# Gate banks of the first three column pairs copied at once, raw weights loaded two pairs ahead, and down weights scaled apart from their splits, in a decoder layer on one core

## Chip, cores and metric

The kernel runs on one core of a Trainium2 chip. The metric is the device time of one execution in microseconds (us); lower is better. Three runs of the kernel before gave 1916.0, 1916.4 and 1918.68 us, median 1916.4.

## What is computed

A decoder layer on 1024 tokens of width 1024 in float32: an attention mixer and a SwiGLU feed-forward, each followed by a residual and a layer norm. The change lies in the feed-forward and in the layer norm just ahead of it.

```python
D_MODEL, SEQ, D_FF = 1024, 1024, 2816

def swiglu(u, w_gate_up, w_down):
    h = jnp.einsum('btd,df->btf', u, w_gate_up)
    hg, hu = jnp.split(h, 2, axis=-1)
    return jnp.einsum('btf,fd->btd', jax.nn.silu(hg) * hu, w_down)

def reference(...):
    ...
    x = layer_norm(DEEPNORM_ALPHA * x + (1.0 + gate_m) * y, ln1_g[l], ln1_b[l])
    u = x * (1.0 + scale_f) + shift_f
    y = swiglu(u, w_gate_up[l], w_down[l])
    return layer_norm(DEEPNORM_ALPHA * x + (1.0 + gate_f) * y, ln2_g[l], ln2_b[l])
```

## The kernel before

**Split operands.** TensorE multiplies in a reduced float32 form, so each operand is held as a high part and a low part. ScalarE copies the source to the high part (L112, L73, L1042), VectorE subtracts to get the low part (L113, L74, L1043), and a product takes three matmuls: high by high, high by low, low by high. Every split is thus one ScalarE and one VectorE instruction on the same tile.

**Gate and up.** The hidden width of 2816 is worked through in 22 pairs p of 128 gate columns and 128 up columns. Gate and up together, for the two halves of the tokens and the two halves of the width, make a 2x2 block product, and it is done with seven products of blocks in place of eight (a form of Strassen's scheme). The names of the seven moving operands are, in order of i = 0 to 6: b11, b21, t2, t1, t3, b22, t4. Each product is 12 matmuls of 128x512 (`product`, L1102). The products accumulate in three PSUM banks in the order a, b, a, c, a, c, a, so bank a is written at i = 0, 2, 4 and 6. Between two of these its value so far has to be read out: ScalarE copies it after i = 0 and after i = 2 (L1236), after i = 4 (L1244), and bank c after i = 3 (L1244). Bank b is added by VectorE at i = 1 (L1247) and a Silu follows (L1248). At i = 6 VectorE multiplies gate by up twice (L1252, L1253), and two stores put the hidden activations into DRAM (`h_d`, L1255).

**Weights of a pair.** `g_load(p)` loads two raw tiles of 512 KB, r1 and r2, two buffers each (L1060, L1064). `g_sums(p, ·)` makes the sums on GpSimd: s1 (L1076), s2 (L1078), a new r2 (L1080), and, when split (p,5) is prepared, a new r1 (L1082). `g_split` splits the right one for each product, some two products ahead. From p = 2 on the next pair's load is written at i = 2 of the current pair, for p = 1 at i = 0; pair 1's own load is early.

**The first three pairs.** Products i = 0 and 1 of pairs 0, 1 and 2 run early, between the last tiles of the layer norm, and leave their sums in six banks. While they run, the second half of the normalized input is transposed (`late_input(k)`, k = 0 to 3), and operands t2, t1, t3, b22 and t4 are made from it piece by piece on ScalarE, VectorE and GpSimd (`late_rest`). Then the loop over p starts and does i = 2 to 6 of pairs 0, 1 and 2, and all seven from pair 3. In it, bank a of a pair is copied only when that pair's turn comes. Tiles of the pool x2p are in use up to the end of pair 0; the pool ev takes that memory from pair 1 on.

**The change of phase.** In pair 21 the loop begins on the down projection: `h_load(f)` loads hidden tiles back, `h_prepare(f)` splits them, and `ws.step()` does a piece of the down weights: GpSimd scales it (L68), ScalarE and VectorE split it (L73, L74). The pieces have three raw buffers, of which each is sent again once its split is done.

**Gain.** In pairs 3 to 10, at i = 6, GpSimd applies the first layer norm's gain and bias to one tile (`gain`, L1023, L1024), from the tile gb1, which is loaded ahead of the layer norm (L961).

**Order.** The schedule is manual: every engine runs its instructions in the order in which the code writes them, and waits for each in turn.

## Time and profile before

| | |
|---|---|
| median of three runs | 1916.4 us |
| the profiled execution | 1917.84 us |
| its span in the trace | 1916.0 us |
| PE (TensorE) busy in the span | 1844.8 us, 96% |
| DVE (VectorE) busy | 1180.4 us, 62% |
| ACT (ScalarE) busy | 781.3 us, 41% |
| POOL (GpSimd) busy | 605.2 us, 32% |
| mean granted TensorE clock | 0.988 |

PE is the engine that decides here. What is to be found is therefore the time in which PE does not run or runs at a lower granted clock. The views for that are the busy time by stage with the granted clock, PE's waits with the line that released each, and the timeline of PE and of the engine that released it. In the timeline a bracket gives the idle time ahead of an instruction and what ended it. Consecutive matmuls overlap, so their spacing, not their duration, is what one costs.

### The profile page before, as it was taken

The page shows a single profiled execution, that of the slowest core. Times are in us where ns is not written, and L with a number is a line of the kernel's source. Part 1 is how long each engine was busy: PE and PEld are TensorE (multiplying, and loading weights), DVE is VectorE, ACT ScalarE, POOL GpSimd, SP SyncE. Part 2 cuts the span into 40 slices and gives each one's busy share as a digit, 9 for nine tenths or more (in the row PEclk, how much of TensorE's full clock was granted, in tenths as well). Part 3 has the DMA queues.
Part 4 walks back from the last instruction along what each step waited for, and adds up shares of the span by engine and source line. Part 5 has one row for each costly group of instructions (what it writes and reads, how often), then busy time and mean ns, then how long its engine had stood idle before and what let it go on. Part 6 is the DMA issues. An engine that isn't in the chain of part 4 may idle for free.

```text
span 1916.0 us, 24451 instructions
## 1 busy us (share of the span) xinstructions
PE 1844.8 (96%) x8988; PEld 1489.2 (78%) x8988; DVE 1180.4 (62%) x2157; ACT 781.3 (41%) x1661; POOL 605.2 (32%) x393
## 2 busy tenths in 40 slices
PE   6899999999999999989999999979999999999998
PEld 5688877878878767768888878758888888788886
DVE  7755667667677887534455365656766445575557
ACT  3455545445444767633122132643333333422122
POOL 2332223223323222000222141635665434431213
PEclk9899999999999999999999999989999999999999
DMA  8011112111121222255434133112222222442222
GB/s 320 22 34 34 40 38 76 46 57 56 41 67 45 58 83 71 74 191 167 167 127 141 60 108 107 56 66 72 94 70 95 72 94 72 149 141 96 95 75 88
DMA packets 72266, 170.83 MB, mean 89 GB/s; under 512 B 13073, under 2 KB 14161, under 8 KB 72146
## 3 DMA queue, kind: packets, MB, share of 16 engines
q1 hardware_dynamic: 71810, 168.21, 26.3%
q8 instruction: 71, 1.16, 0.2%
q0 software_dynamic: 336, 1.06, 0.2%
q14 instruction: 49, 0.40, 0.1%
HBM read 145.80 MB, written 23.43 MB: 88 GB/s over the span
## 4 chain that ended last, share of the span: by engine, by line
PE 50%; DVE 3%; issue 1%; ACT 1%; DMA 1%; POOL 0%; SPq 0%; DVEq 0%; POOLq 0%; ACTq 0%
PE pf L1102 20%; PE p L133 5%; PE p L134 5%; PE p L132 5%; PE pf L133 5%; PE pf L134 5%; PE pf L132 5%; DVE m L113 1%; DMA h_raw<-h_d 0%; DVE w_lo L113 0%; DMA r<-in_w_gate_up 0%; ACT w_hi L112 0%; DMA w_raw<-in_w_down 0%; POOL w_raw L68 0%; DVE t3l L1043 0%
## 5 line engine op out<-in xcount | busy, mean ns | idle before, releaser
L132 PE MATMUL pj<-u,w_hi 128*128 128x512 f32 x720 | 300.9, 418 | 0.0
L134 PE MATMUL pj<-u,w_lo 128*128 128x512 f32 x720 | 283.5, 394 | 0.0
L133 PE MATMUL pj<-u,w_hi 128*128 128x512 f32 x720 | 282.3, 392 | 0.0
L420 POOL TENSOR_TENSOR rb<-rb,sin_t 128x512 f32<-128x512 f32 x64 | 86.8, 1356 | 502.1 <-DVE rb L418 431.5
L113 DVE TENSOR_TENSOR w_lo<-r,w_hi 128x512 fp32r<-128x512 f32 x110 | 99.9, 917 | 143.3 <-ACT w_hi L112 143.3
L74 DVE TENSOR_TENSOR w_lo<-w_raw,w_hi 128x512 fp32r<-128x512 f32 x150 | 133.2, 891 | 83.0 <-ACT w_hi L73 80.7
L523 ACT ACTIVATE probs<-probs,st 128x128 f32<-128x128 f32 (+1 forms) x320 | 146.1, 461 | 60.7 <-DVE st L513 31.0
L132 PEld LDWEIGHTS pj<-u,w_hi 128*128 128x128 f32 x720 | 136.1, 189 | 33.5 <-issue 4.7
L134 PEld LDWEIGHTS pj<-u,w_lo 128*128 128x128 f32 x720 | 135.7, 188 | 30.6
L133 PEld LDWEIGHTS pj<-u,w_hi 128*128 128x128 f32 x720 | 136.3, 189 | 22.5
L133 PE MATMUL pf<-wd,h 128*128 128x512 f32 x352 | 137.0, 389 | 0.6 <-DVE wd L74 0.6
L132 PE MATMUL pf<-wd,h 128*128 128x512 f32 x352 | 137.2, 390 | 0.0
L134 PE MATMUL pf<-wd,h 128*128 128x512 f32 x352 | 137.0, 389 | 0.0
L68 POOL TENSOR_TENSOR w_raw<-w_raw,gate 128x512 f32<-128x512 f32 x60 | 84.6, 1426 | 155.6 <-DMA w_raw<-in_w_down 141.5
L1307 DVE SCALAR_TENSOR_TENSOR zt<-zt,pf 128x512 f32<-128x512 f32 x112 | 76.0, 686 | 80.2 <-PE pf L134 80.2
L421 POOL TENSOR_TENSOR r<-ra,rb 128x512 f32<-128x512 f32 x63 | 114.5, 1818 | 6.1 <-DVE kl L455 1.3
L73 ACT ACTIVATE w_hi<-w_raw 128x512 fp32r<-128x512 f32 x150 | 92.0, 624 | 29.0 <-PE p L133 12.0
L547 ACT ACTIVATE ptsb<-pt 128x512 f32<-128x512 f32 (+1 forms) x128 | 63.6, 548 | 93.5 <-PE pt L545 93.1
L132 PE MATMUL p<-u,w_hi 128*128 128x512 f32 x224 | 88.3, 394 | 0.0
L134 PE MATMUL p<-u,w_lo 128*128 128x512 f32 x224 | 87.2, 389 | 0.0
L133 PE MATMUL p<-u,w_hi 128*128 128x512 f32 x224 | 87.2, 389 | 0.0
L132 PE MATMUL p<-o_hl,w_hi 128*128 128x512 f32 x192 | 75.8, 395 | 6.1 <-ACT o_hl L112 6.1
(293 smaller groups left out, 4323.7 us busy)
## 6 DMA issues: line engine op xcount, KB each, us to landing
w_raw<-in_w_in SPq DMA_DIRECT2D x118, 256.0 KB
r<-in_w_gate_up SPq DMA_DIRECT2D x47, 512.0 KB
a_raw<-in_w_ada SPq DMA_DIRECT2D x32, 512.0 KB
w_raw<-in_w_down SPq DMA_DIRECT2D x44, 256.0 KB
h_raw<-h_d SPq DMA_DIRECT2D x22, 512.0 KB
h_d<-g SPq DMA_DIRECT2D x42, 256.0 KB
wa<-in_w_ada_m SPq DMA_DIRECT2D x16, 512.0 KB
wb<-wt_d SPq DMA_DIRECT2D x24, 256.0 KB
```

The source lines that it names most:

```text
L68: self.nc.gpsimd.tensor_tensor(raw, raw, scale(), op=OP.mult)
L73: self.nc.scalar.activation(hi, raw, AF.Copy)
L74: self.nc.vector.tensor_tensor(lo, raw, hi, op=OP.subtract)
L113: nc.vector.tensor_tensor(lo, src, hi, op=OP.subtract)
L132: nc.tensor.matmul(ps, w[0], m[0], start=first, stop=False)
L133: nc.tensor.matmul(ps, w[0], m[1], start=False, stop=False)
L134: nc.tensor.matmul(ps, w[1], m[0], start=False, stop=last)
L420: eng.tensor_tensor(b, b, sin_t[:, s], op=OP.mult)
L421: eng.tensor_tensor(residue_half(res, r, t), by_residue(a, r), by_residue(b, r), op=OP.add)
L523: nc.scalar.activation(pr, pr, AF.Exp, bias=st[:, 0, h, b:b + 1], accum_out=st[:, 1, h, b:b + 1])
L1102: nc.tensor.matmul(ps, w[:, c], m[:, k], start=first and k == 0 and n == 0, stop=k == 3 and n == 2, skip_group_check=True)
L1307: nc.vector.scalar_tensor_tensor(z, z, ALPHA if gi == 0 else 1.0, pd, op0=OP.mult, op1=OP.add)
```

## The change

The added function `early_gate(p)` copies bank a of pair p on ScalarE, and adds bank b on VectorE, at once after those banks are complete. It is called for pair 0 after `late_input(0)`, for pair 1 after `late_input(2)`, and for pair 2 at p = 0, i = 2. At i = 0 and 1 of those pairs the copy and the add are then left out; the Silu stays. The results lie in a weight buffer (pair 0) and in a new tile `spare`, which takes the memory of gb1; gb1 is loaded in pair 3 instead. The last two tiles of `late_input` go into `spare` too.

Four subtractions that make raw21 (the source of t4) go from GpSimd to VectorE, between the four low parts of b22.

`g_load(p + 2)` is written at i = 4 of every pair, `g_sums(p + 1, ·)` at i = 2, 3 and 4.

The scaling of a down piece is a method of its own. Three pieces are sent at p = 20, i = 5 and scaled at p = 21, i = 0; the splits are spread over i = 2, 3, 5 and 6.

```diff
+    def scale(self, i):
+        scale = self.jobs[i][2]
+        if scale is not None and i not in self.scaled:
+            self.nc.gpsimd.tensor_tensor(self.raws[i], self.raws[i], scale(), op=OP.mult)
+            self.scaled.add(i)
...
     def step(self):
...
         self.send()
-        _, kh, scale, dest = self.jobs[i]
+        self.scale(i)
+        _, kh, _, dest = self.jobs[i]
         raw = self.raws.pop(i)
-        if scale is not None:
-            self.nc.gpsimd.tensor_tensor(raw, raw, scale(), op=OP.mult)
...
-    gb1 = norm_params(1)
...
+    spare = misc.tile([P, 4, TH], F32, name="spare", tag="gb")
+    late, gated = {}, {}
...
         elif name == "t3":
             split_to("t3", k, r12)
-            nc.gpsimd.tensor_tensor(raw21[:, k], raw21[:, k], raw_t2[:, k], op=OP.subtract)
...
+    def early_gate(p):
+        gated[p] = wpool.tile([P, TH], F32, name="w_raw", tag="w_raw", bufs=3) if p == 0 else spare[:, p - 1]
+        nc.scalar.activation(gated[p], acc[p][0], AF.Copy)
+        nc.vector.tensor_tensor(gated[p], gated[p], acc[p][1], op=OP.add)
...
         if k == 1:
             g_split(0, 2)
+        if k in (0, 2):
+            early_gate(k // 2)
...
             if p == 0 and i == 2:
                 late_rest("t3", 0)
+                early_gate(2)
...
             if i in (0, 2):
-                g[i // 2] = kept("g")
-                nc.scalar.activation(g[i // 2], x, AF.Copy)
+                g[i // 2] = gated.get(p) if i == 0 else None
+                if not g[i // 2]:
+                    g[i // 2] = kept("g")
+                    nc.scalar.activation(g[i // 2], x, AF.Copy)
...
             if i in (1, 5):
                 t = i // 5
-                nc.vector.tensor_tensor(g[t], g[t], x, op=OP.add)
+                if t or p not in gated:
+                    nc.vector.tensor_tensor(g[t], g[t], x, op=OP.add)
                 nc.scalar.activation(g[t], g[t], AF.Silu)
...
             if p == 0 and i in (3, 4):
                 for k in range(4):
+                    if i == 3:
+                        nc.vector.tensor_tensor(raw21[:, k], raw21[:, k], raw_t2[:, k], op=OP.subtract)
                     late_rest({3: "b22", 4: "t4"}[i], k)
             if p + 1 < NF:
-                if i == (2 if p >= EARLY_PAIRS - 1 else 0) and p:
-                    g_load(p + 1)
-                if i in ((3, 4, 5) if p >= EARLY_PAIRS else (2, 3, 4)):
-                    g_sums(p + 1, i - (3 if p >= EARLY_PAIRS else 2))
+                if i == 4 and p + 2 < NF:
+                    g_load(p + 2)
+                if i in (2, 3, 4):
+                    g_sums(p + 1, i - 2)
+                if p == NF - 2 and i == 5:
+                    ws.limit = None
+                    ws.send()
             else:
                 if i == 0:
-                    ws.limit = None
-                    ws.send()
-                if i == 1:
                     h_load(0)
                     h_load(1)
+                    for j in range(3):
+                        ws.scale(len(ws.done) + j)
                 if i in (2, 3, 4):
                     h_prepare(i - 2)
-                    if i < 4:
-                        h_load(i)
+                    if i == 2:
+                        h_load(2)
+                for _ in range({2: 2, 3: 1, 5: 1, 6: 2}.get(i, 0)):
                     ws.step()
-                    ws.step()
+            if p == EARLY_PAIRS and i == 0:
+                gb1 = norm_params(1)
```

In the rows of the instruction order that follow, a line number under "now" is that of the changed file, 4 to 13 higher.

**ScalarE, from the last `late_input` to product t2 of pair 0.** Here `px` is a transposed tile, `pf` a bank, and w_hi the high part of a weight. Before:

```order
L1031 ACTIVATE w_raw<-px,lnpp 128x512 x2
L1042 ACTIVATE t2h<-raw_t_10490 128x512
L1042 ACTIVATE t1h<-raw_10063 128x512 x2
L112 ACTIVATE w_hi<-s_10418 128x512
L1236 ACTIVATE w_raw<-pf 128x512
L1248 ACT_TABLE_LOAD
L1248 ACTIVATE w_raw<-w_raw 128x512
L1042 ACTIVATE t3h<-r 128x512
L1236 ACTIVATE r<-pf 128x512
L1042 ACTIVATE t3h<-r 128x512 x2
```

Now:

```order
L1046 ACTIVATE t1h<-raw_10060 128x512
L1174 ACTIVATE spare<-pf 128x512
L1035 ACTIVATE spare<-px,lnpp 128x512 x2
L1046 ACTIVATE t2h<-raw_t_10487 128x512
L1046 ACTIVATE t1h<-raw_10060 128x512 x2
L117 ACTIVATE w_hi<-s_10415 128x512
L1261 ACT_TABLE_LOAD
L1261 ACTIVATE w_raw<-w_raw 128x512
L1046 ACTIVATE t3h<-r 128x512
L1174 ACTIVATE spare<-pf 128x512
L1248 ACTIVATE r<-pf 128x512
```

The copies of the banks of pairs 1 and 2 stand among the operands' copies, pair 0's stands some rows above, and the table load and the Silu follow the weight split directly.

**VectorE, products t3 to t4 of pair 0**, from the low part of t3's weights. Before:

```order
L113 TENSOR_TENSOR w_lo<-r_10353,w_hi 128x512
L113 TENSOR_TENSOR w_lo<-r_10351,w_hi 128x512
L1043 TENSOR_TENSOR b22l<-r,b22h 128x512 x3
L1043 TENSOR_TENSOR b22l<-w_raw,b22h 128x512
L113 TENSOR_TENSOR w_lo<-r_10353,w_hi 128x512
L1043 TENSOR_TENSOR t4l<-raw_10064,t4h 128x512 x4
L113 TENSOR_TENSOR w_lo<-s_10704,w_hi 128x512
```

Now:

```order
L118 TENSOR_TENSOR w_lo<-r_10350,w_hi 128x512
L118 TENSOR_TENSOR w_lo<-r_10348,w_hi 128x512
L1272 TENSOR_TENSOR raw_10061<-raw_10061,raw_t_10487 128x512
L1047 TENSOR_TENSOR b22l<-r,b22h 128x512
L1272 TENSOR_TENSOR raw_10061<-raw_10061,raw_t_10487 128x512
L1047 TENSOR_TENSOR b22l<-r,b22h 128x512
L1272 TENSOR_TENSOR raw_10061<-raw_10061,raw_t_10487 128x512
L1047 TENSOR_TENSOR b22l<-r,b22h 128x512
L1272 TENSOR_TENSOR raw_10061<-raw_10061,raw_t_10487 128x512
L1047 TENSOR_TENSOR b22l<-spare,b22h 128x512
L118 TENSOR_TENSOR w_lo<-r_10350,w_hi 128x512
L1047 TENSOR_TENSOR t4l<-raw_10061,t4h 128x512 x4
```

The four subtractions that make raw21 (here `raw_1006…`) stand between the low parts of b22.

**SyncE, pairs 0 to 2** (both pieces begin with the two loads of pair 1; the first two stores into `h_d` are pair 0's, the next two pair 1's; each further two loads are those of the next pair). Before:

```order
L1060 DMA r_10523<-in_w_gate_up 128x1024
L1064 DMA r_10525<-in_w_gate_up 128x1024
L1255 DMA h_d<-w_raw 128x512
L1255 DMA h_d<-r 128x512
L1060 DMA r_10807<-in_w_gate_up 128x1024
L1064 DMA r_10809<-in_w_gate_up 128x1024
L1255 DMA h_d<-g 128x512 x2
L1060 DMA r_10935<-in_w_gate_up 128x1024
L1064 DMA r_10937<-in_w_gate_up 128x1024
```

Now:

```order
L1064 DMA r_10521<-in_w_gate_up 128x1024
L1068 DMA r_10523<-in_w_gate_up 128x1024
L1064 DMA r_10762<-in_w_gate_up 128x1024
L1068 DMA r_10764<-in_w_gate_up 128x1024
L1268 DMA h_d<-w_raw 128x512
L1268 DMA h_d<-r 128x512
L1064 DMA r_10871<-in_w_gate_up 128x1024
L1068 DMA r_10873<-in_w_gate_up 128x1024
L1268 DMA h_d<-spare 128x512
L1268 DMA h_d<-g 128x512
L1064 DMA r_10976<-in_w_gate_up 128x1024
L1068 DMA r_10978<-in_w_gate_up 128x1024
```

Pair 2's loads stand ahead of pair 0's stores, pair 3's ahead of pair 1's, and so on: each load has moved up by about one pair.

**ScalarE, end of pair 21** (`wd` is a piece of the down weights, `h` a hidden tile, `c` the copies after i = 3 and i = 4). Before:

```order
L73 ACTIVATE wd<-w_raw 128x512 x2
L112 ACTIVATE w_hi<-r_13507 128x512
L1244 ACTIVATE c_13693<-pf 128x512
L112 ACTIVATE h<-h_raw 128x1024
L73 ACTIVATE wd<-w_raw 128x512 x2
L112 ACTIVATE w_hi<-r_13509 128x512
L1244 ACTIVATE c_13727<-pf 128x512
L112 ACTIVATE h<-h_raw 128x1024
L73 ACTIVATE wd<-w_raw 128x512 x2
L1248 ACTIVATE g<-g 128x512
```

Now:

```order
L78 ACTIVATE wd<-w_raw 128x512 x2
L117 ACTIVATE w_hi<-r_13409 128x512
L1256 ACTIVATE c_13691<-pf 128x512
L117 ACTIVATE h<-h_raw 128x1024
L78 ACTIVATE wd<-w_raw 128x512
L117 ACTIVATE w_hi<-r_13411 128x512
L1256 ACTIVATE c_13717<-pf 128x512
L117 ACTIVATE h<-h_raw 128x1024
L1261 ACTIVATE g<-g 128x512
L78 ACTIVATE wd<-w_raw 128x512 x3
```

Ahead of the split of (21,6) and the second c copy stands one piece in place of two, ahead of the Silu none in place of two, and three follow the Silu.

## Rows read from the trace of the kernel before

**Rows 1.** Busy time by stage: pair 0, pair 1, and the stretch from pair 3 on. The columns are the stretch, its length, the busy time (and instructions) of PE, PE's weight loads, DVE, ACT and POOL, the granted TensorE clock, the share of the DMA engines and GB/s.

```profile
1236.00:1262.00 26.00, 19.67 (x62) 14.06 (x60) 20.59 (x23) 14.57 (x26) 15.28 (x10) 0.80 0.00 1
1262.00:1282.00 20.00, 16.14 (x64) 13.11 (x65) 8.50 (x12) 7.89 (x14) 6.83 (x5) 0.91 0.22 79
1301.00:1640.00 339.00, 339.00 (x1490) 278.87 (x1489) 196.35 (x195) 128.30 (x231) 166.66 (x103) 1.00 0.25 84
```

**Rows 2.** Waits of PE from 1236 us to the end of the span: the waiting line, the line it waited for, us in total, times, longest.

```profile
PE pf L1102 <- ACT c L1244: 6.1, 2, 3.3
PE pf L1102 <- ACT g L1236: 4.0, 1, 4.0
PE pf L1102 <- ACT w_raw L1236: 2.7, 1, 2.7
PE pf L1102 <- ACT w_hi L112: 2.1, 1, 2.1
PE pf L1102 <- DVE w_lo L113: 1.4, 1, 1.4
PE pf L133 <- DVE wd L74: 0.6, 1, 0.6
```

**Rows 3.** Timeline of PE, from the last matmul ahead of pair 0's t2 to pair 3: start, duration, operation, and in brackets the idle time ahead and what ended it.

```profile
1235.87 0.39 PE L1102 MATMUL pf<-b21h,w_lo 128*128 128x512 f32 x1
1238.95 0.50 PE L1102 MATMUL pf<-t2h,w_hi 128*128 128x512 f32 x1 [2.70 <-ACT w_raw L1236]
...
1248.68 0.50 PE L1102 MATMUL pf<-t3h,w_hi 128*128 128x512 f32 x1 [2.10 <-ACT w_hi L112]
...
1261.44 0.39 PE L1102 MATMUL pf<-t4h,w_lo 128*128 128x512 f32 x1
1265.86 0.50 PE L1102 MATMUL pf<-t2h,w_hi 128*128 128x512 f32 x1 [4.02 <-ACT g L1236]
...
1273.05 0.39 PE L1102 MATMUL pf<-t3h,w_hi 128*128 128x512 f32 x1
...
1275.77 0.39 PE L1102 MATMUL pf<-b22h,w_hi 128*128 128x512 f32 x1
...
1281.20 0.39 PE L1102 MATMUL pf<-t2h,w_hi 128*128 128x512 f32 x1
...
1292.85 0.50 PE L1102 MATMUL pf<-b22h,w_hi 128*128 128x512 f32 x1 [3.32 <-ACT c L1244]
...
1300.31 0.39 PE L1102 MATMUL pf<-b11h,w_hi 128*128 128x512 f32 x1
```

**Rows 4.** Timeline of DVE in pair 0, from the last piece of `late_input` to the end of t4's low parts (22 instructions in all).

```profile
1234.72 0.68 DVE L1151 TENSOR_TENSOR raw<-w_raw,raw 128x512 f32<-128x512 f32 x1
...
1237.79 3.44 DVE L1043 TENSOR_TENSOR t1l<-raw,t1h 128x512 fp32r<-128x512 f32 x2
...
1250.04 1.28 DVE L113 TENSOR_TENSOR w_lo<-r,w_hi 128x512 fp32r<-128x512 f32 x2
...
1256.59 4.27 DVE L1043 TENSOR_TENSOR t4l<-raw,t4h 128x512 fp32r<-128x512 f32 x4 [2.26 <-ACT t4h L1042]
```

**Rows 5.** Timeline of POOL: the four subtractions in pair 0 (x4 is a group of four), the first sums of pairs 2 and 3, and the r1 sum of pair 4, right behind the first gain.

```profile
1237.28 6.78 POOL L1162 TENSOR_TENSOR raw<-raw,raw_t 128x512 f32<-128x512 f32 x4
...
1271.33 1.29 POOL L1076 TENSOR_TENSOR s<-r 128x512 f32<-128x512 f32 x1 [12.22 <-DMA r<-in_w_gate_up]
...
1289.16 1.27 POOL L1076 TENSOR_TENSOR s<-r 128x512 f32<-128x512 f32 x1 [9.52 <-DMA r<-in_w_gate_up]
...
1324.67 1.74 POOL L1082 TENSOR_TENSOR r<-r,s 128x512 f32<-128x512 f32 x1
```

**Rows 6.** Timeline of SyncE's queue: the issue of pair 2's second raw tile.

```profile
1266.11 0.41 SPq L1064 DMA_DIRECT2D r<-in_w_gate_up  x1
```

**Rows 7.** Timeline of ACT: the table load and the Silu in pair 0, the bank copy of pair 1, the split of (2,5), and the split of (4,5).

```profile
1238.92 1.28 ACT L1248 ACT_TABLE_LOAD   x1
1243.55 0.63 ACT L1248 ACTIVATE w_raw<-w_raw 128x512 f32<-128x512 f32 x1 [3.35 <-DVE w_raw L1247]
...
1265.20 0.60 ACT L1236 ACTIVATE g<-pf 128x512 f32<-128x512 f32 x1 [1.96 <-DVE r L1253]
...
1291.68 0.63 ACT L112 ACTIVATE w_hi<-r 128x512 fp32r<-128x512 f32 x1 [6.71 <-POOL r L1082]
...
1329.12 0.62 ACT L112 ACTIVATE w_hi<-r 128x512 fp32r<-128x512 f32 x1
```

**Rows 8.** Timeline of POOL and ACT at the end of pair 21.

```profile
1660.91 1.26 POOL L68 TENSOR_TENSOR w_raw<-w_raw,gate 128x512 f32<-128x512 f32 x1 [5.45 <-DMA w_raw<-in_w_down]
1662.20 0.63 ACT L73 ACTIVATE wd<-w_raw 128x512 fp32r<-128x512 f32 x1 [3.45 <-POOL w_raw L68]
...
1663.26 0.58 ACT L1244 ACTIVATE c<-pf 128x512 f32<-128x512 f32 x1
```

**Rows 9.** Timeline of PE at the same place, from t4 of pair 21 to the first matmuls of the down phase.

```profile
1663.89 0.50 PE L1102 MATMUL pf<-t4h,w_hi 128*128 128x512 f32 x1 [2.81 <-ACT c L1244]
...
1669.40 0.50 PE L133 MATMUL pf<-wd,h 128*128 128x512 f32 x1 [0.63 <-DVE wd L74]
```

**Rows 10.** Timeline of ACT early in the span: the other load of a table set, and the instruction behind it.

```profile
53.61 1.28 ACT L307 ACT_TABLE_LOAD   x1
54.90 1.15 ACT L307 ACTIVATE sin_t<-ang,freq 128x1024 f32<-128x1024 f32 x1
```

More of the change, by code (lines that the diff above doesn't have):

```diff
@@ L46, in __init__ @@
         self.jobs, self.raws, self.done, self.sent, self.used = [], {}, [], 0, 0
-        self.limit = None
+        self.limit, self.scaled = None, set()
     def add(self, src, kh, scale=None, dest=None):
@@ L1019, in normalize, with gain @@
         nc.scalar.activation(z, z, AF.Identity, bias=rs[:, 1:2], scale=rs[:, 0:1])
-    def gain(tb):
+    def gain(tb, gb1):
         nc.gpsimd.tensor_tensor(zrow(tb), zrow(tb), gb1[:, 0], op=OP.mult)
@@ L1141, in decoder_layer @@
     raw_t2 = low.tile([P, 4, TH], F32, name="raw_t2", tag="big")
-    late = {}
+    spare = misc.tile([P, 4, TH], F32, name="spare", tag="gb")
+    late, gated = {}, {}
     def late_input(k):
-        r12, r22 = [wpool.tile([P, TH], F32, name="w_raw", tag="w_raw", bufs=3) if k == 3 else
-                    x2p.tile([P, TH], F32, name="r", tag="r", bufs=6) for _ in range(2)]
+        r12, r22 = [spare[:, 2 + i] if k == 3 else x2p.tile([P, TH], F32, name="r", tag="r", bufs=6) for i in range(2)]
         turned(r12, 1, k)
@@ L1217, in kept @@
                 return ev.tile([P, TH], F32, name=name, bufs=4 if name == "g" else 1)
-            if not g[0]:
-                return wpool.tile([P, TH], F32, name="w_raw", tag="w_raw", bufs=3)
             return x2p.tile([P, TH], F32, name="r", tag="r", bufs=6)
@@ L1257, in decoder_layer @@
                 for k in range(4):
+                    if i == 3:
+                        nc.vector.tensor_tensor(raw21[:, k], raw21[:, k], raw_t2[:, k], op=OP.subtract)
                     late_rest({3: "b22", 4: "t4"}[i], k)
             if p + 1 < NF:
-                if i == (2 if p >= EARLY_PAIRS - 1 else 0) and p:
-                    g_load(p + 1)
-                if i in ((3, 4, 5) if p >= EARLY_PAIRS else (2, 3, 4)):
-                    g_sums(p + 1, i - (3 if p >= EARLY_PAIRS else 2))
+                if i == 4 and p + 2 < NF:
[5 more added lines that the diff above has]
+                    ws.send()
             else:
                 if i == 0:
-                    ws.limit = None
-                    ws.send()
-                if i == 1:
                     h_load(0)
                     h_load(1)
+                    for j in range(3):
+                        ws.scale(len(ws.done) + j)
                 if i in (2, 3, 4):
                     h_prepare(i - 2)
-                    if i < 4:
-                        h_load(i)
+                    if i == 2:
+                        h_load(2)
+                for _ in range({2: 2, 3: 1, 5: 1, 6: 2}.get(i, 0)):
                     ws.step()
-                    ws.step()
+            if p == EARLY_PAIRS and i == 0:
+                gb1 = norm_params(1)
             if i == 6 and EARLY_PAIRS <= p < EARLY_PAIRS + NB:
-                gain(p - EARLY_PAIRS)
+                gain(p - EARLY_PAIRS, gb1)
     gb2 = norm_params(2)
```

## Prediction

> **What bounds the kernel now.** PE is busy for 96% of the span, so the first view to read is the busy time by stage, with the granted clock [rows 1]. From pair 3 on PE is busy for the whole of 339 us at full clock: nothing that other engines do there can help. In pair 0 it is busy for 19.67 of 26 us at a mean granted clock of 0.80 (between the levels of 2.4 and 1.2 GHz), in pair 1 for 16.14 of 20 us at 0.91. The second view, PE's waits behind that point, names all that is left [rows 2]: six groups, 16.5 us of idle time. The third, PE's timeline, says where they stand [rows 3, 9] and gives the yardstick: an undisturbed product, t3 of pair 1, takes 1275.77 - 1273.05 = 2.72 us, five of them 13.6 us.
>
> With it the loss of each pair can be counted, idle time and low clock together. Each pair ends where the next begins; a full-speed matmul is 2.72/12 = 0.23 us apart from the next [rows 3].
> - Pair 0: from 1236.10 to 1261.67, 25.57 us, so 12.0 us lost. The waits are 2.70 for the copy of bank a, 2.10 for the high part of t3's weights, and 1.4 for their low part [rows 2, 3]. The other 5.8 us is almost all low clock.
> - Pair 1: 1261.67 to 1281.20, 19.53 us, 5.9 lost: 4.02 us of waiting for the copy of bank a, the rest low clock.
> - Pair 2: 1281.20 to 1300.31, 19.11 us, 5.5 lost: 3.32 us of waiting for the c copy, the rest low clock.
> - End of pair 21: 2.81 us of waiting for the c copy, and 0.63 for a low part of the down weights [rows 9], some 4.2 us in all with the restart of the pipeline and the spacing about them.
>
> That is 27.6 us. All of the change's gain must come from it.
>
> **The change, part by part.**
>
> *Pair 1, bank a.* The copy waited until VectorE had finished the last multiply of pair 0 (1265.20, released by L1253), since its tile lies in memory that pair 0 still used [rows 7]. The early copy lies in another tile and is done before the loop. The wait and the low clock behind it go: 5.9 us. What is late next is the copy after t2 (i = 2), which still goes into that memory; t3 needs it. If pair 0 ends at about 1259 to 1260, the multiply ends near 1263 and t3 begins at 1260 + 2 x 2.72 = 1265, so 1 to 2 us is left.
>
> *Pair 2, loads.* Pair 2's second raw tile was issued at 1266.11 [rows 6] and the first sum on it began at 1271.33: 5.2 us from issue to use [rows 5]. Pair 3's came so late that its first sum (1289.16) held up the r1 sum of pair 2, which stands behind it on POOL. The split of (2,5) waited 6.71 us for that sum [rows 7], and the c copy that released PE stands behind the split on ACT. With loads one pair earlier the whole chain is early. Pair 2's loads now wait for the splits of (0,5) and (0,6), near 1258; 1258 + 5.2 = 1263, then two sums of 1.3 us, and b22 of pair 1 begins at 1260 + 3 x 2.72 = 1268. It holds, with about 2 us to spare. 5.5 us goes in pair 2. For both pairs I take **11.4 us**; if one of these two margins fails, some 3 us with its low clock comes back.
>
> *Pair 0.* Three bank copies in place of one and two more adds now stand among the operand work. The first wait (2.70) goes. What remains is the row of VectorE's work. A low part takes 0.64 us where POOL is idle (1250.04: two in 1.28) and 1.72 us where POOL works beside it (1237.79: two in 3.44), 1.1 more [rows 4]. Before, 22 VectorE instructions and 10 of POOL [rows 1, 4] make 22 x 0.61 + 10 x 1.1 = 24.4 us (0.61 is the spacing); the trace has 26.1 us from 1234.72 to 1260.86. Now there are 26 (four subtractions more; the add of pair 0 goes, that of pair 2 comes) and 6: 15.9 + 6.6 = 22.5 us. With the same 1.7 us of rest, and a start 0.7 later for the add of pair 1, it ends at 1259.6, 1.3 us earlier. Moving the subtractions off POOL [rows 5] is thus a saving of 4 x (1.1 - 0.61) = 2.0 us, of which the adds take a part. Followed by hand, instruction by instruction, the low part of t3's weights comes at about 1247.5 in place of 1250.7, 3.2 us earlier, and if PE's clock stays up, up to 4.7. At the other end the gain is nothing, if the low parts of t4 still set the end. I take **2.3 us**, midway between 1.3 and 3.2; bounds 0 and 4.7.
>
> *The table load.* It took 1.28 us on ACT inside a wait of 3.35 us for VectorE [rows 7], so it cost nothing. Now it stands ahead of a Silu that waits for nothing, and the split of t3's weights comes behind it. Its 1.28 us is in the walk above, where VectorE is mostly later than ACT. The other load in this trace also takes 1.28 us, and the next instruction starts 1.29 us after it [rows 10]. The Trainium skill, page "ScalarE: Activation LUTs", section "What ACT_TABLE_LOAD costs", speaks against putting it there: to a load of 1283 ns it adds a drain of some 1380 ns, 2.66 us in all. The rows show the load and no drain; by that page the sum would be an estimated 1.4 us smaller, if ACT decides.
>
> *End of pair 21.* ACT's c copy stood behind a split that waited for a POOL scaling, which began at 1660.91 after 5.45 us of waiting for its data [rows 8]. That split is now behind the Silu. The copy can run right after t3, and t4 begins at 1660.9: 3.0 us. But the down phase then starts 3 us earlier, and the last pieces do not come earlier: the piece behind the one that came at 1660.91 must still be scaled, split, and its low part stands behind two multiplies on VectorE. From the same rows I put it at 1665.5 to 1668, needed at 1665.2. So 0.3 to 2.6 us of a new wait stand against 4.2 us lost now: a gain of 1.6 to 3.9. I take **2.2 us**, nearer to the low end since the present run also waits for such a piece.
>
> *The rest, at nothing.* gb1's load at pair 3 has 16 us until the first gain. In all pairs from 3 on, POOL now does the first sum of the next pair ahead of the r1 sum of this one. Behind the first gain that r1 sum ended at 1326.4, and its split began at 1329.12 [rows 5, 7]: one sum of 1.3 us more fits, and PE needs it only at 1333. PE has no wait there now, so nothing can be gained.
>
> **Sum.** 11.4 + 2.3 + 2.2 = 15.9 us. The profiled execution was 1917.84 us with a span of 1916.0; its span would be 1900.1. It lies 1.4 us above the median of 1916.4, so the forecast against the median is 1916.4 - 15.9 = **1900.5 us**.
>
> **Rivals.**
> - *Pair 0 opens up.* If VectorE's row is not what binds, pair 0 gains 4.7 us or more, and the change of phase 3.9: 20.0 us, 1896.4. For it: VectorE stood idle 2.26 us ahead of t4's low parts [rows 4]. Against it: the same count of instructions explains 24.4 of 26.1 us.
> - *New waits.* The margins of pairs 1 and 2 are 1 to 2 us, and the waits of 4.02 and 3.32 us were each followed by a stretch of low clock worth some 2 us (5.9 - 4.0, 5.5 - 3.3). If one margin fails in each pair, 3 + 3 us comes back, and pair 0 gives nothing: 15.9 - 6 - 2.3 = 7.6 us, 1908.8.
> - *The table load lands on the path.* If ACT, and not VectorE, decides when t3's weights come, the load's 1.28 us [rows 7, 10] comes off pair 0's 2.3 us: 1901.8. For it: PE's wait ahead of t3 was first one for ACT, 2.10 us [rows 3]. Against it: the wait for VectorE's low part came later still. With the drain of the page "ScalarE: Activation LUTs" of the Trainium skill (section "What ACT_TABLE_LOAD costs") this case would give an estimated 1903.2.
> - *The change doesn't do what it says.* If VectorE's and ACT's rows in pair 0 grow by what the copies add, and the waits of pairs 1 and 2 only change their names (the c copy's tile in place of the gate's), the time stays within 0.2%, about 1914.
> - *Slower.* POOL's new order is the mechanism: the first sum of pair p+1 stands ahead of the r1 sum of p, behind a gain, in eight pairs. It may overwrite its tile only after the split of (p,3). From the end at 1326.4 plus 1.3 to PE's need at 1333 there are about 4 us of room, with the split in between. If the sum came 4 + 2 = 6 us late in each, 8 x 2 = 16 us would eat the gain; at 7 us late the kernel would take 1916.4 - 15.9 + 8 x 3 = 1924.5.
>
> **How the numbers follow.** The forecast has 0.53, pair 0 opening 0.13, new waits 0.15, the table load 0.07, no effect 0.07, slower 0.05. A difference of 0.2%, 3.8 us here, is about what a measurement of this kernel can tell from no change. Faster by more than that are the first four, 0.88; within it 0.07; slower 0.05. The range runs from 1896.0, where pair 0 opens, to 1908.5, close to where the new waits all come; what is left out is about 0.15 to 0.2.
>
> **What would show it.** In PE's timeline of the changed kernel t2 of pair 0 should follow the last b21 without a wait; t2 of pair 1 and b22 of pair 2 should have none, and pairs 1 and 2 should take 13.6 us each. Pair 0 should end at about 1259 with a wait for t3's weights left. t4 of pair 21 should follow b22 at once, with a wait of 0.3 to 2.6 us for a low part of the down weights in the down phase. POOL's first sums should no longer wait for loads from pair 3 on. The prediction is wrong if PE waits anywhere between pairs 3 and 20, if pair 1 waits for the copy after t2, or if pair 0 ends before 1257 or after 1262.

## The result, and the profile after

The changed kernel took 1902.3 us (median of five runs, 1899.23 to 1908.77) against 1916.0 of the kernel before beside it: a ratio of 0.9932, 95% interval 0.991 to 0.9954, or 13.0 us less by that ratio (8.8 to 17.2; the two medians differ by 13.7). A second set of five runs gave 1901.05 us and 0.9922 (0.9908 to 0.9936). The forecast was 1900.5 us. The time was forecast well; pair 0, the end of pair 21 and the pairs from 3 on were not, and their errors have opposite signs.

The trace of the changed kernel is that of its slowest run (1908.77 us, span 1907.0). First view: busy time by stage, with the columns of [rows 1]; the stretches are pair 0, pairs 1 and 2, and pair 3 to the end of b22 of pair 21.

```profile
1237.75:1259.36 21.61, 17.48 (x61) 12.79 (x60) 18.09 (x27) 15.44 (x28) 11.18 (x6) 0.84 0.14 49
1259.36:1286.56 27.20, 27.20 (x121) 22.53 (x120) 18.04 (x17) 12.14 (x22) 16.14 (x11) 1.00 0.33 117
1286.56:1645.61 359.05, 359.05 (x1586) 297.40 (x1585) 193.39 (x212) 140.73 (x249) 174.41 (x112) 1.00 0.27 89
```

Pairs 1 and 2 lose nothing: 27.20 us for ten products of 2.72, at full clock. Pair 0 is shorter, but still at a mean granted clock of 0.84. Next, PE's waits from 1200 us on, which answer [rows 2]:

```profile
PE pf L137 <- DVE zt L1326: 2.9, 1, 2.9
PE pf L1106 <- ACT w_hi L117: 2.1, 1, 2.1
PE pf L138 <- DVE wd L79: 1.9, 1, 1.9
PE pf L1106 <- DVE w_lo L118: 1.9, 2, 1.4
...
PE pf L137 <- ACT wd L78: 0.5, 1, 0.5
```

The waits for bank copies, for the c copies and for the loads behind them are all gone. t3's two waits in pair 0 have stayed. Three waits are left in the down phase, where the kernel before had one of 0.6 us [rows 2]: two for pieces of the down weights (`wd`), and one, for `zt` (VectorE's add that empties a finished bank), of a new kind. PE's timeline shows where they stand; it answers [rows 3, 9].

```profile
1237.52 0.39 PE L1106 MATMUL pf<-b21h,w_lo 128*128 128x512 f32 x1
1237.74 0.39 PE L1106 MATMUL pf<-t2h,w_hi 128*128 128x512 f32 x1
...
1246.81 0.50 PE L1106 MATMUL pf<-t3h,w_hi 128*128 128x512 f32 x1 [2.14 <-ACT w_hi L117]
...
1248.90 0.80 PE L1106 MATMUL pf<-t3h,w_lo 128*128 128x512 f32 x1 [1.35 <-DVE w_lo L118]
...
1259.36 0.39 PE L1106 MATMUL pf<-t2h,w_hi 128*128 128x512 f32 x1
...
1650.34 0.50 PE L137 MATMUL pf<-wd,h 128*128 128x512 f32 x1 [0.49 <-ACT wd L78]
...
1652.78 0.50 PE L138 MATMUL pf<-wd,h 128*128 128x512 f32 x1 [1.94 <-DVE wd L79]
...
1668.24 0.79 PE L137 MATMUL pf<-wd,h 128*128 128x512 f32 x1 [2.88 <-DVE zt L1326]
```

With the boundaries of PE's timeline, every kernel of this study can be taken apart in the same way: a pair ends one spacing (0.23) after the start of its last matmul of t4, pair 0 starts one spacing after that of the last b21, and the "end" runs from one spacing after the start of the last matmul of b22 of pair 21 to the end of the span. Times in us; "(1)" is one run.

| kernel | time | pair 0 starts | pair 0 | pair 1 | pair 2 | end |
|---|---|---|---|---|---|---|
| before | 1916.0 | 1236.10 | 25.57 | 19.53 | 19.11 | 255.1 |
| before_again | 1914.83 (1) | 1232.80 | 25.58 | 19.52 | 19.24 | 255.1 |
| changed | 1902.3 | 1237.75 | 21.62 | 13.60 | 13.60 | 261.4 |
| after_again | 1901.05 | 1232.79 | 21.52 | 13.59 | 13.60 | 257.2 |
| e1_h3_early | 1899.35 | 1234.88 | 21.48 | 13.60 | 13.60 | 255.4 |
| e2_old_end | 1897.74 | 1234.98 | 21.45 | 13.60 | 13.60 | 255.8 |
| e3_gate0_only | 1908.66 | 1232.18 | 20.96 | 19.50 | 13.64 | 259.4 |
| e4_old_loads | 1914.88 | 1233.04 | 21.75 | 19.52 | 19.04 | 259.2 |
| e5_subs_pool | 1901.61 (1) | 1234.45 | 24.03 | 13.94 | 13.60 | 254.8 |
| e6_no_gate0 | 1900.21 (1) | 1234.88 | 21.08 | 14.24 | 13.60 | 255.5 |
| e7_table_early | 1899.25 (1) | 1234.82 | 21.27 | 13.60 | 13.60 | 255.2 |
| e8_t3_weights_first | 1898.04 | 1233.63 | 20.27 | 14.27 | 13.60 | 255.4 |
| e9_end_steps | 1896.8 | 1232.35 | 20.29 | 14.24 | 13.60 | 254.0 |
| e10_best | 1898.13 | 1233.53 | 20.22 | 14.26 | 13.60 | 254.0 |

Two things help in reading it. The start of pair 0 varies by 5.6 us, between two traces of the same kernel by 3.3 and 5.0: that is a large part of the noise of the time, and it arises ahead of everything that the change touches: VectorE's first instruction on `zt`, which comes 220 us ahead of the old place of gb1's load, is at 902.98 and 899.59 us in the two traces of the kernel before, at 904.13 and 899.45 in those of the changed kernel. The stages of the two kernels that were traced twice repeat within 0.15 us, but for the end of the changed kernel.

Between before_again and after_again, which start alike, the stages give 4.1 + 5.9 + 5.6 - 2.1 = 13.5 us; the spans differ by 1913.0 - 1897.8 = 15.2. The rest, 1.7 us, is in pairs 4 to 11, in which the forecast saw nothing to gain: see the fourth point below.

### The profile page after: what moved, and what is told of

Read it like the earlier page. It is cut to its first block, busy times and chain, and to the rows that moved or that the text cites. A ratio compares the mean times of both kernels' runs of the same rounds, so it can differ in the third digit from the quotient of the medians.

```text
span 1907.0 us, 24471 instructions
## 1 busy us (share of the span) xinstructions
PE 1841.1 (97%) x8988; PEld 1489.6 (78%) x8988; DVE 1160.4 (61%) x2161; ACT 782.0 (41%) x1661; POOL 596.5 (31%) x389
## 4 chain that ended last, share of the span: by engine, by line
PE 51%; DVE 3%; ACT 1%; issue 1%; DMA 1%; SPq 0%; POOL 0%; DVEq 0%; ACTq 0%; POOLq 0%
PE pf L1106 21%; PE p L138 5%; PE p L139 5%; PE p L137 5%; PE pf L137 5%; PE pf L139 5%; PE pf L138 5%; DVE m L118 1%; DMA h_raw<-h_d 0%; DVE wd L79 0%; DVE h L118 0%; DMA oa_d<-o 0%; PE px L1034 0%; PE p L835 0%; PE p L842 0%
## 5 line engine op out<-in xcount | busy, mean ns | idle before, releaser
L118 DVE TENSOR_TENSOR w_lo<-r,w_hi 128x512 fp32r<-128x512 f32 x110 | 117.7, 1072 | 138.7 <-ACT w_hi L117 137.9
L137 PE MATMUL pf<-wd,h 128*128 128x512 f32 x352 | 139.2, 395 | 3.4 <-DVE zt L1326 2.9
L138 PE MATMUL pf<-wd,h 128*128 128x512 f32 x352 | 138.7, 394 | 1.9 <-DVE wd L79 1.9
L139 PE MATMUL pf<-wd,h 128*128 128x512 f32 x352 | 138.6, 394 | 0.0
```

The source lines that it names most:

```text
L118: nc.vector.tensor_tensor(lo, src, hi, op=OP.subtract)
L137: nc.tensor.matmul(ps, w[0], m[0], start=first, stop=False)
L138: nc.tensor.matmul(ps, w[0], m[1], start=False, stop=False)
L139: nc.tensor.matmul(ps, w[1], m[0], start=False, stop=last)
```

## The experiments

**The load of hidden tile 3.** The new wait for `zt` is the first thing to explain. Timelines of SyncE, ACT and DVE in the changed kernel:

```profile
1655.56 0.43 SPq L921 DMA_DIRECT2D gb<-in_ln_b  x1
1656.03 1.15 SPq L1212 DMA_DIRECT2D h_raw<-h_d  x2
...
1664.07 1.06 ACT L117 ACTIVATE h<-h_raw 128x1024 fp32r<-128x1024 f32 x1 [13.03 <-DMA h_raw<-h_d]
...
1665.16 1.23 DVE L118 TENSOR_TENSOR h<-h_raw,h 128x1024 fp32r<-128x1024 f32 x1 [11.83 <-ACT h L117]
...
1667.51 2.47 DVE L1326 SCALAR_TENSOR_TENSOR zt<-zt,pf 128x512 f32<-128x512 f32 x4
```

The load is issued behind the gain's loads; ACT waits 13 us for it, VectorE 11.8 for ACT, and four finished banks wait behind VectorE's split. Kernel e1 undoes this alone, kernel e2 the whole new order at the end.

```diff
-                    if i == 2:
-                        h_load(2)
+                    if i < 4:
+                        h_load(i)
```

> The changed kernel with the load of hidden tile 3 written at i = 3 of pair 21 again, as in the kernel before. Theory: in the changed kernel this load comes only after the last stores and the two loads of the second norm's gain; VectorE's split of tile 3 then waits 11.8 us, the adds of the first finished banks stand behind it, and PE waits 2.9 us for a bank with some 2.8 us of low clock behind it. Then that wait goes here and the time falls by about 5.5 us against the changed kernel, to about 1897 us. Rival: the wait belongs to the one profiled run, or comes from the phase's earlier start whatever the place of the load: then PE waits for a bank here too, or the time stays at about 1902 us.

> The changed kernel with the whole change of phase (sends, scalings, splits and loads of pairs 20 and 21) as in the kernel before. Theory: the wait of 2.8 us ahead of t4 of pair 21 comes back, and the three waits of the first 20 us of the down phase (0.5, 1.9 and 2.9 us, with low clock) go; the end costs 4.2 us as before in place of some 9 us, so the time is some 5 us under the changed kernel, about 1897 us. Rival (the prediction's term): the new order at the end saves 2.2 us, so undoing it costs that much, about 1904.5 us.

Measured: e1 1899.35 us, ratio 0.9908 (0.9893 to 0.9923), e2 1897.74 us, 0.9905 (0.9891 to 0.9918). The wait for `zt` is absent from both. The load in e1's timeline, and its split, which now waits for nothing:

```profile
1639.27 0.33 SPq L1212 DMA_DIRECT2D h_raw<-h_d  x1
...
1650.25 1.21 DVE L118 TENSOR_TENSOR h<-h_raw,h 128x1024 fp32r<-128x1024 f32 x1
```

The times are 3 to 4.6 us under the changed kernel's, and 1.7 to 3.3 under its second set, less than the 5.5 and 5 that were expected from the first trace; the intervals of the ratios overlap with the changed kernel's, so it is the traces, not the times, that show the effect. The end takes 255.4 and 255.8 us, 255.1 before: with the early load, the rest of the new order neither gains nor loses. Was the wait an accident of that trace?

> The changed kernel once more, word for word. If the wait for a bank in the down phase belongs to its instruction order, PE waits 2.5 to 4 us for VectorE's add near the tenth microsecond of that phase here too, and the time is 1901 to 1904 us, 3 to 5 us above the kernels e1_h3_early and e2_old_end. If it belonged to the first profiled run alone, the wait is absent and the time is 1898 to 1900 us.

Measured: 1901.05 us, and PE waits for `zt` again, for 1.5 us:

```profile
PE pf L137 <- DVE zt L1326: 1.5, 1, 1.5
```

In e3 and e4, which have the same end, it is 3.6 and 3.8 us:

```profile
PE pf L137 <- DVE zt L1325: 3.6, 1, 3.6
```

```profile
PE pf L137 <- DVE zt L1326: 3.8, 1, 3.8
```

It belongs to the order. What the end loses goes with the moment at which ScalarE can split tile 3: 14.4, 14.8, 15.0 and 15.8 us after the first matmul of the down phase (after_again, e3, e4, changed), with ends of 257.2, 259.4, 259.2 and 261.4 us. The wait alone does not tell the loss: in e3 PE came to the bank sooner, since its granted clock was 1.00 in the 4 us behind the wait of 1.9 us, and 0.62 in after_again. Why the tile's moment varies was not settled.

**Early copies or early loads.** Kernel e3 calls `early_gate(0)` alone, kernel e4 puts loads and sums back to their old places.

```diff
-        if k in (0, 2):
-            early_gate(k // 2)
+        if k == 0:
+            early_gate(0)
...
-                early_gate(2)
```

> The changed kernel with the early bank copy and add for pair 0 alone; pairs 1 and 2 copy theirs in their own turn. Theory: PE waits some 4 us ahead of t2 of pair 1 again, with low clock behind it, 5.9 us in all: about 1908 us. Rival: with pair 0 shorter and the loads early, the copy of pair 1 finds its tile free in time, and the time stays at about 1902 us.

```diff
-                if i == 4 and p + 2 < NF:
-                    g_load(p + 2)
-                if i in (2, 3, 4):
-                    g_sums(p + 1, i - 2)
+                if i == (2 if p >= EARLY_PAIRS - 1 else 0) and p:
+                    g_load(p + 1)
+                if i in ((3, 4, 5) if p >= EARLY_PAIRS else (2, 3, 4)):
+                    g_sums(p + 1, i - (3 if p >= EARLY_PAIRS else 2))
```

> The changed kernel with raw weights loaded one pair ahead and their sums made at the places of the kernel before. Theory: PE waits some 3.3 us ahead of b22 of pair 2 (or of pair 1, which now begins earlier) for the c copy behind a split that waits for POOL, with low clock behind it: 5.5 us or more, about 1908 us. Rival: the loads are not what matters once the banks are free: about 1902 us.

Measured: e3 1908.66 us (0.9964; 0.9949 to 0.9978), e4 1914.88 us (0.9992; 0.9983 to 1.0001). PE's waits of e3, then of e4:

```profile
PE pf L1106 <- ACT g L1247: 4.0, 1, 4.0
```

```profile
PE pf L1106 <- ACT c L1256: 7.3, 2, 4.1
```

In e3 pair 1 takes 19.50 us, as before. In e4 it takes 19.52 too, though its bank is copied early, and the time is 1914.88 and not the 1908 that were expected: the wait has moved three products on, to b22, where the c copy stands behind a split that waits 7.7 us for GpSimd. ACT's timeline of e4:

```profile
1266.02 0.63 ACT L117 ACTIVATE w_hi<-r 128x512 fp32r<-128x512 f32 x1 [7.71 <-POOL r L1086]
1266.55 0.58 ACT L1256 ACTIVATE c<-pf 128x512 f32<-128x512 f32 x1
```

So pair 1 had two stalls of 5.9 us, one hidden by the other, and only both edits together free it. Pair 2 needs the loads alone; e4 moves them together with their sums, and no run parts the two. Without the loads, the whole change gives 0.1%, which can't be told from nothing: pair 0 of e4 is 3.8 us shorter than before, but its end is 4.1 us longer.

**What binds pair 0.** Three kernels, all with the old end, each change one thing: e5 puts the four subtractions back on GpSimd, e6 leaves the early copy of pair 0 out, e7 loads the table set early.

```diff
             split_to("t3", k, r12)
+            nc.gpsimd.tensor_tensor(raw21[:, k], raw21[:, k], raw_t2[:, k], op=OP.subtract)
...
-                    if i == 3:
-                        nc.vector.tensor_tensor(raw21[:, k], raw21[:, k], raw_t2[:, k], op=OP.subtract)
```

> The kernel with the old change of phase (e2_old_end), with the four subtractions that make raw21 back on GpSimd. Read by the length of pair 0 in PE's timeline, which is 21.5 us in the runs so far. The prediction's theory: VectorE's row, slowed by 1.1 us for each instruction of GpSimd beside it, binds pair 0; then pair 0 grows by some 2 us, and the low part of t1's last weights comes some 2 us later. Rival: the row of ScalarE ahead of t3's weights binds, and pair 0 stays within 0.5 us of 21.5.

```diff
-        if k in (0, 2):
-            early_gate(k // 2)
+        if k == 2:
+            early_gate(1)
...
+            if not g[0]:
+                return wpool.tile([P, TH], F32, name="w_raw", tag="w_raw", bufs=3)
```

> The kernel with the old change of phase, without the early copy of pair 0; pairs 1 and 2 keep theirs. Theory: the wait of about 2.7 us ahead of t2 of pair 0 comes back with its low clock, pair 0 takes 24 to 26 us, and pairs 1 and 2 stay at 13.6 us each. Rival: the gain of 4 us in pair 0 came from the subtractions alone, and pair 0 stays at 21.5 to 22.5 us.

```diff
+        if k == 1:
+            dummy = misc.tile([P, 1], F32, name="dummy")
+            nc.scalar.activation(dummy, ident[:, 0:1], AF.Silu)
```

> The kernel with the old change of phase, with a Silu of one column written into late_input(1), ahead of its first split, so that the table load falls there, in a wait of ScalarE. If the load lies on the path to t3's weights (a rival of the prediction), PE's wait ahead of t3 shrinks from 2.2 us to about 0.9 and pair 0 by 1.3 us or more; if VectorE decides, the wait for the low part of those weights grows by as much and pair 0 stays at 21.5 us.

Measured, pair 0: 24.03, 21.08 and 21.27 us, against 21.45 of e2. PE's waits between 1225 and 1300 us, of e5, e6 and e7 in turn:

```profile
PE pf L1106 <- DVE w_lo L118: 5.6, 2, 3.8
```

```profile
PE pf L1106 <- ACT w_raw L1250: 3.3, 1, 3.3
```

```profile
PE pf L1106 <- DVE w_lo L118: 2.9, 2, 2.3
PE pf L1106 <- ACT w_hi L117: 0.8, 1, 0.8
```

In e5 the wait has gone from the bank copy to the low part of t1's weights, because VectorE again works beside GpSimd there. DVE and POOL of e5:

```profile
1236.85 3.44 DVE L1047 TENSOR_TENSOR t1l<-raw,t1h 128x512 fp32r<-128x512 f32 x2
1240.21 1.75 DVE L118 TENSOR_TENSOR w_lo<-s,w_hi 128x512 fp32r<-128x512 f32 x1
```

```profile
1236.33 6.76 POOL L1166 TENSOR_TENSOR raw<-raw,raw_t 128x512 f32<-128x512 f32 x4
```

In the changed kernel the two t1l take 1.28 us. The subtractions are worth 2.6 us. The early copy of pair 0 is worth little beside them: in e6 PE waits 3.3 us ahead of t2, and then hardly at all; pair 0 is 0.4 us shorter, and pair 1 0.6 us longer. The rival that was written for e6 holds, though the wait that its theory named is there. Counted against the kernel before, pair 0 gains 25.57 - 24.03 = 1.5 us with the copy and without the subtractions (e5), 4.5 with the subtractions and without the copy (e6; 3.9 after what pair 1 gives back), 4.1 with both.

In e7 the wait for the high part of t3's weights falls from 2.2 to 0.8 us, and that for the low part grows from 1.3 to 2.3. Pair 0 gains 0.2 us: the table load is not on the path.

Kernel e8 writes the split of t3's weights ahead of the Silu and the copies.

```diff
     g_split(0, 3)
+    g_split(0, 4)
...
-    prepared = [2]
+    prepared = [3]
```

> The kernel with the old change of phase, with the split of t3's weights of pair 0 written right after that of t1's, ahead of the Silu and the copies of t3's operands. Theory: PE's wait of 2.2 and 1.3 us ahead of t3 and the low clock behind it go; then VectorE's row, which ends some 2 us ahead of the present end of pair 0, binds: pair 0 takes 19 to 20 us in place of 21.5, and the time is some 2 us under that of e2_old_end, about 1896 us. Rival: the operands' copies are what is late, and pair 0 stays at 21.5 us.

Measured: 1898.04 us, 0.9913 (0.99 to 0.9927), and pair 0 at 20.27 us, of which 0.7 comes back in pair 1. Pair 0 comes close to the 19 to 20 us of the theory, the time does not show it: 0.5 us net is far under the noise.

**Two attempts to do better.** Kernel e9 joins e1 and e8 and splits two pieces of down weights ahead of the last Silu. Kernel e10 adds the early table load and moves `early_gate(2)` to the end of pair 0.

```diff
-                for _ in range({2: 2, 3: 1, 5: 1, 6: 2}.get(i, 0)):
+                for _ in range({2: 2, 3: 1, 4: 2, 6: 1}.get(i, 0)):
```

> The kernel e1_h3_early (new change of phase, hidden tile 3 loaded early) with two pieces of the down weights split at i = 4 of pair 21, ahead of the last Silu, in place of one at i = 5 and one more at i = 6, and with the split of t3's weights first as in e8_t3_weights_first. If the place of these splits behind the Silu and VectorE's multiplies makes the waits of 0.5 and 1.9 us in the down phase, they shrink to 1 us or less, and with 1.2 us from pair 0 the time is 1896 to 1897 us, the lowest of all. If GpSimd's scaling of those pieces, which cannot begin before their data come, makes them, the waits stay and the time is about 1898 us.

```diff
-                early_gate(2)
...
+            if p == 0 and i == 6:
+                early_gate(2)
```

> e9_end_steps with the table load in late_input(1), as in e7_table_early, and with pair 2's early copy and add at the end of pair 0 in place of i = 2. Theory: with the split of t3's weights first, ScalarE's first copy for t3 comes 1.3 us earlier, VectorE's row loses one add of 0.6 us and a wait of about 1.1, and pair 0 shrinks from 20.3 to 18.5 to 19.5 us, the time to about 1895.5 us. Rival: the bank copy that t3 waits for still stands behind VectorE's first low part of t3, slowed by GpSimd, and pair 0 stays at 20 us.

Measured: e9 1896.8 us, 0.9899 (0.9885 to 0.9913); e10 1898.13 us, 0.9903 (0.9886 to 0.9919). At the end e9 gains 1.4 us on e1 (254.0 against 255.4). PE's two waits there:

```profile
1645.32 0.50 PE L138 MATMUL pf<-wd,h 128*128 128x512 f32 x1 [1.06 <-DVE wd L79]
1648.97 0.50 PE L138 MATMUL pf<-wd,h 128*128 128x512 f32 x1 [1.28 <-DVE wd L79]
```

They are 2.3 us together, hardly less than the 0.5 and 1.9 of e1; what is gone is the low clock behind them. The 4 us behind the longest wait of e1, then of e9 (the first bracket is PE's matmuls, the third value from the right the granted clock):

```profile
1649.78:1653.78 4.00, 4.00 (x11) 3.18 (x12) 2.17 (x3) 0.63 (x1) 1.45 (x1) 0.62 0.96 301
```

```profile
1648.97:1652.97 4.00, 4.00 (x18) 3.31 (x19) 3.85 (x4) 0.63 (x1) 1.62 (x1) 1.00 0.90 246
```

So the new place of the splits did not take the waits away. In e9's trace the split of the first piece waits 1.6 us for GpSimd's scaling, and the low part of the second stands behind VectorE's multiply: both causes that were named are there.

In e10 pair 0 stays at 20.22 us, as its rival said, but not for the rival's reason: the wait for the bank copy ahead of t3 has shrunk from 1.6 us (e9) to 0.4, and the waits have moved on to the low parts of t3 (1.2) and b22 (1.4 in four). VectorE's row is the bound there. Kernels e1, e2, e8, e9 and e10 can't be told apart by their times; the medians of all lie below the changed kernel's.

> The kernel before, word for word, for a second trace of it. Expected: pair 0 25.6 us, pair 1 19.5, pair 2 19.1, and 255.1 us from the end of b22 of pair 21 to the end, each within 0.2 us of the first trace; what varies is the start of pair 0, between 1232 and 1238 us in all kernels of this study. If the start varies no more than 0.5 us here and is at 1236, the early load that the change removes would cost about 2 us, which no term of the prediction has.

Measured: pair 0 25.58, pair 1 19.52, pair 2 19.24, end 255.1 us, and a start of pair 0 at 1232.80, 3.3 us earlier than in the first trace of the same kernel. No cost or gain of the removed early load can be seen in it.

## Why the prediction came out as it did

**Pairs 1 and 2, 11.4 us: right.** Both took 13.60 us, as forecast. One thing was not seen. The text gave pair 1's loss to the bank copy and pair 2's to the loads, and checked only that the new loads reach b22 of pair 1 in time. e3 and e4 show that pair 1 had both stalls, so that neither edit alone gains its 5.9 us.

**Pair 0, 2.3 us: right in kind, too small; 4.0 measured (bounds 0 and 4.7).** The failed step is the count of VectorE's row. It charged 1.1 us for each of six instructions of GpSimd and kept 1.7 us of rest, and put the end of the row at 1259.6 us on a start of 1235.4. In the changed trace the row begins at 1237.04 and t4's low parts are done at 1257.27, that is 20.2 us and not 24.2:

```profile
1237.04 0.68 DVE L1155 TENSOR_TENSOR raw<-spare,raw 128x512 f32<-128x512 f32 x1
...
1254.79 2.48 DVE L1047 TENSOR_TENSOR t4l<-raw,t4h 128x512 fp32r<-128x512 f32 x4
```

The 26 instructions at 0.61 make 15.9 us of it and the waits for ScalarE 2.6 (0.70, 1.22 and 0.64), which leaves some 1.8 us for GpSimd, where the text had charged 6.6. The four low parts of t4 took 2.48 us, 4.27 before [rows 4], though GpSimd had an instruction under way; the charge per instruction is not a constant.

Nor did the end of the row set the end of pair 0: PE waits for nothing after t3's weights, and pair 0 ends at 1259.36, 2.1 us after the row. What set it is the low part of t3's weights and the granted clock of 0.50 (the level of 1.2 GHz) in the 5.3 us behind that wait. The walk by hand put this low part 3.2 us earlier; measured from the start of pair 0, PE's matmul with it came 14.7 - 11.2 = 3.5 us earlier (1250.78 - 1236.10, 1248.90 - 1237.75), most of the 4.0. Before:

```profile
1250.78 0.79 PE L1102 MATMUL pf<-t3h,w_lo 128*128 128x512 f32 x1 [1.36 <-DVE w_lo L113]
```

The walk was the better method. That VectorE's row binds is shown for the low parts of t1's and t3's weights (e5, e7), and for those of t3 and b22 once the waits ahead of them are shorter (e10). The price of the subtractions was right in size, 2.0 us forecast and 2.6 measured.

**End of pair 21, a gain of 2.2 us: wrong; a loss of 2.1 and 6.3 us in the two traces.** Its first half was right: t4 follows b22 at once, 3.0 us, and the new waits of the down phase, 0.5 and 1.9 us, lie, taken together, within the forecast 0.3 to 2.6. Two steps failed. The first is that the new waits were charged without the low clock behind them: in e1, where they are all that is left, the granted clock behind the longer one is 0.62, and the end takes 255.4 us, 0.3 more than before and not 2.2 less. The second is that no price was given to the load of hidden tile 3. The diff takes it from i = 3 of pair 21 to behind the last stores and the gain's loads, and the text says nothing of it, although its split stands ahead of the adds that free PE's banks. By the traces of e1 (255.4) and of the changed kernel (257.2 and 261.4) it costs 1.8 and 6.0 us.

**"The rest, at nothing": wrong by some 1.5 us, to the good.** The text read "PE busy for the whole of 339 us" as no loss. But eight pairs, those whose t2 falls behind a gain, took 19.23 us and the others 19.04: 8 x 0.19, some 1.5 us. The matmuls overlap, so a shift of 0.2 us leaves no idle time. Here is the place in pair 4, of the kernel before: PE, then VectorE.

```profile
1325.02 0.39 PE L1102 MATMUL pf<-t2l,w_hi 128*128 128x512 f32 x1
1325.31 0.50 PE L1102 MATMUL pf<-t2h,w_lo 128*128 128x512 f32 x1
1325.64 0.39 PE L1102 MATMUL pf<-t2h,w_hi 128*128 128x512 f32 x1
```

```profile
1322.36 2.90 DVE L113 TENSOR_TENSOR w_lo<-s,w_hi 128x512 fp32r<-128x512 f32 x1
```

The third matmul comes 0.06 us late and the one behind it 0.10, since the low part of t2's weights was done only at 1325.26: it took 2.90 us beside the gain on GpSimd, whose second half began at 1321.97, and the r1 sum that followed it at 1324.67 [rows 5]:

```profile
1321.97 2.74 POOL L1024 TENSOR_TENSOR zt<-zt,gb 128x1024 f32<-128x1024 f32 x1
```

After, VectorE and then GpSimd:

```profile
1309.68 1.28 DVE L118 TENSOR_TENSOR w_lo<-s,w_hi 128x512 fp32r<-128x512 f32 x2
```

```profile
1306.48 2.73 POOL L1028 TENSOR_TENSOR zt<-zt,gb 128x1024 f32<-128x1024 f32 x1
...
1311.04 1.29 POOL L1080 TENSOR_TENSOR s<-r 128x512 f32<-128x512 f32 x1 [1.83 <-DVE w_lo L118]
```

With the sums earlier, the gain now ends at 1309.21, 0.5 us ahead of the first split; before, it ended 2.3 us after that split had begun. GpSimd's next instruction behind the gain is now the first sum, which must wait for that very split; while it waits, VectorE is alone, and its two splits take 1.28 us. It is so in all eight pairs, and all pairs take 19.04 us. In e4, with the old order of sums and the old loads, the eight take 19.19 to 19.27 again. The rival that feared this order ("slower", 0.05) had the place right and the sign wrong.

**The rivals.** The table load is not on the path (e7). New waits did take the place of old ones, but at the end, not in pairs 1 and 2. Pair 0 did not open by the 4.7 us of that rival: it gained 4.0. With the split of t3's weights moved as well (e8) it gained 5.3, of which pair 1 gave back 0.7; VectorE's row then holds it at 20.2 us (e10). That the forecast of the time came so near is in part luck: its errors cancel, too little by 1.7 us in pair 0 and some 1.5 in the steady pairs, too much by 4.3 to 8.5 at the end.

## What to carry to other kernels

List every DMA that a diff moves, and ask what stands behind its consumer on each engine: here a load for the next group of products, 144 matmuls or 33 us away, held four PSUM banks, through a split ahead of the adds that empty them. Where a stall is taken away, look for the next one at the same place by removing each edit in turn: a pair with two stalls shows only the one that comes first. And a tensor engine that is busy for 100% of a stretch can still lose time; compare the spacing of equal pieces of work, not the busy share.

## What the runs showed of the hardware that had not been expected

- VectorE and GpSimd slow each other, but not always both. In e5 three VectorE instructions took about 1.7 us each beside four of GpSimd at 1.7 each. In e8, while VectorE issued a dense row at 0.60 us spacing, one addition on GpSimd of 128x512, 1.29 us alone, took 6.92 us (4.79 in the changed kernel), and VectorE was not slowed. What decides which of them gives way was not settled.

```profile
1247.87 6.92 POOL L1264 TENSOR_TENSOR r<-r 128x512 f32<-128x512 f32 x1 [5.28 <-ACT r L1257]
```

- The table load cost 1.28 us and no more where it stood in a chain. In the changed kernel the Silu begins 1.29 us after it:

```profile
1240.76 1.28 ACT L1261 ACT_TABLE_LOAD   x1
1242.05 0.63 ACT L1261 ACTIVATE w_raw<-w_raw 128x512 f32<-128x512 f32 x1
```

  The Trainium skill, page "ScalarE: Activation LUTs", section "What ACT_TABLE_LOAD costs", adds a drain of some 1380 ns; no row here shows it.

- The same wait was followed by a low clock in one run and not in another: after the wait of 1.65 us ahead of t3, the granted clock of the next stretch was 0.53 in e8 (near the lower level, 1.2 GHz) and 1.00 in e9, which runs the same instructions there. Pair 0 took 20.27 and 20.29 us: there, where PE had to wait for VectorE a few products on, the low clock cost nothing. The stretches of e8, then of e9:

```profile
1243.40:1247.00 3.60, 3.55 (x9) 2.77 (x10) 3.60 (x7) 3.60 (x8) 0.00 (x0) 0.53 0.14 42
```

```profile
1242.10:1245.70 3.60, 2.87 (x12) 2.09 (x12) 3.60 (x8) 3.60 (x8) 0.00 (x0) 1.00 0.22 51
```
